# First loads of a two-block kernel in smaller pieces on two queues

## The chip, the cores and the metric

The kernel runs on one core of one Trainium2 chip. The metric is the device time of one execution in microseconds (us). A profiled execution gives a trace of every engine's instructions and of the DMA packets; its times count from the start of the span, the stretch from the first to the last instruction.

## The reference

The reference computes two transformer-like blocks on 256 tokens of width 1024, in float32, and a last norm. What matters here is the first work that the kernel does, the keys and values of the memory attention in the first block:

```
m = rms_norm(mem, mem_norm[l])                 # mem: 256 x 1024
mk, mv = jnp.split(m @ w_mem_kv[l], 2, axis=-1)
```

and what rms_norm is:

```
y = x32 * lax.rsqrt(jnp.mean(x32 * x32, axis=-1, keepdims=True) + EPS)
return (y * gain.astype(jnp.float32)).astype(x.dtype)
```

Everything after it (the recurrent, linear-attention and memory branches, both feed-forward parts, the second block) is untouched by the change.

## The kernel before

All activations lie with channels on the 128 partitions: mem is a tile memr of 128 x 8 x 256, channel tile k of 8 against 256 tokens. Weights lie in one packed array; the chunk memk0 is 8 channel tiles by 256 output columns, so 2048 numbers per partition, and memk1 and memk2 follow it.

Products are made three times over: every operand is split into a high part (rounded to the format that TensorE takes) and a low part (the rest). The helper split has ScalarE write the high part (line 156, or line 159 with a scale) and VectorE the low part (line 157 or 160). The helper mm3 issues high x high, high x low and low x high (lines 203 to 205). For mem the scale is the norm's gain, 8 columns named g_mem in the parameter tile par; the 1/rms of each token is worked out beside the products and multiplied in afterwards.

The opening goes as follows. A tile of ones is written; the first 16 columns of par (g_mem and g_mix) are loaded on ScalarE's queue; 13 products of ones by ones (line 258) run on TensorE before there is data. Then a loop over four quarters q loads on SP's queue two channel tiles of mem (mem_part, line 344) and the matching quarter of memk0 and of memk1 (512 columns each, line 363), splits each, and issues the 24 products of the quarter into two accumulators, fps[0] and fps[1]. Behind the loop come memk2 in quarters (line 191), the constants, the squares of mem (Ssq.add, lines 282 and 290), their fold (line 292), the column sums on TensorE (line 297), an inverse square root on VectorE (lines 306 to 321), and memk2's products. After that, weights are loaded in whole chunks (line 178), three raw buffers ahead.

The order written in the program is a priority. When the kernel is built, a planner puts each engine's instructions in an order by its own estimate of readiness, and so a square of mem can stand ahead of a weight's split that the program writes earlier. An engine keeps this order at run time, whatever is ready. In the trace the ninth load waits, at its issue, for the first one, that of the scales, to land.

Of the kernel before, what the change touches and what calls it, by code (L numbers as in the profile page):

```python
# [9 lines left out]
F32 = mybir.dt.float32  # L10
# [7 lines left out]
P = 128  # L18
D = 1024
S = 256  # L20
KT = D // P
# [25 lines left out]
NPAR = _o  # L47
# [18 lines left out]
WMAX = KT * 272  # L66
# [21 lines left out]
def wplan():  # L88
    plan = []
    for n in ("memk", "memv", "mq", "zrnn"):  # L90
        plan += [(f"{n}{j}", KT, 256) for j in range(3)]
    plan += [(f"qk{j}", KT, 256) for j in range(3)]
    plan += [("rga", 14, 128), ("rgx", 14, 128)]
    plan += [("v0", KT, 272), ("v1", KT, 256), ("v2", KT, 256)]
    plan += [(f"g{j}", KT, 256) for j in range(3)]
    for b in BR_ORDER:
        for j in range(4):
            plan += [(f"gate{b}_{j}", KT, 256), (f"br{b}_{j}", MT, 256)]
    plan += [(f"wout{j}", KT, 256) for j in range(4)]
    plan += ffn_plan("up", "dn", NF)  # L100
    plan += [(n, KT, IN2_WIDTH.get(n, 256)) for n in IN2_ORDER]
    plan += [(f"wo2_{j}", 2, 1024) for j in range(4)]
    plan += ffn_plan("gu", "dn2_", NF2)
    off = {}
    o = 0
    for n, a, b in plan:
        off[n] = (o, a, b)
        o += P * a * b
    return off, o


WOFF, WTOT = wplan()
# [3 lines left out]
def build(ctx: ExitStack, tc: tile.TileContext, ins: dict, out: bass.AP):  # L116
    nc = tc.nc
    act, dve, pool, pe = nc.scalar, nc.vector, nc.gpsimd, nc.tensor
    W = ins["w"]

    wrp = ctx.enter_context(tc.tile_pool(name="wrp", bufs=3))
    whp = ctx.enter_context(tc.tile_pool(name="whp", bufs=5))
    wlp = ctx.enter_context(tc.tile_pool(name="wlp", bufs=5))
    cp = ctx.enter_context(tc.tile_pool(name="cp", bufs=1))
# [8 lines left out]
    def uid(p):  # L133
        cnt[0] += 1
        return f"{p}_{cnt[0]}"

    def t2(shape=None, dt=F32):
        return tp.tile(shape or [P, 512], dt, tag="t2", name=uid("t2"))

    def slot(tag, shape, dt=F32):  # L140
        return sp.tile(shape, dt, tag=tag, name=uid(tag))

    def small(shape):
        n = uid("sm")
        return sm.tile(shape, F32, tag=n, name=n)

    def bank(shape=None):
        return psp.tile(shape or [P, 2, 256], F32, tag="ps", name=uid("ps"))
# [5 lines left out]
    def split(dst_h, dst_l, src, scale=None):  # L154
        if scale is None:
            act.activation(dst_h, src, AF.Copy)  # L156
            dve.tensor_tensor(dst_l, src, dst_h.bitcast(F32), op=ALU.subtract)  # L157
        else:
            act.activation(dst_h, src, AF.Identity, scale=scale)
            dve.scalar_tensor_tensor(dst_l, src, scale, dst_h.bitcast(F32),  # L160
                                     op0=ALU.mult, op1=ALU.subtract)
# [3 lines left out]
    raws = {}  # L165
# [36 lines left out]
    def mm3(o, lh, ll, rh, rl, start, stop, skip=False):  # L202
        pe.matmul(o, lh, rh, start=start, stop=False, skip_group_check=skip)  # L203
        pe.matmul(o, lh, rl, start=False, stop=False, skip_group_check=skip)  # L204
        pe.matmul(o, ll, rh, start=False, stop=stop, skip_group_check=skip)  # L205
# [43 lines left out]

    ones = cp.tile([P, P], F32, name="ones")  # L250
    dve.memset(ones, 1.0)
    par = cp.tile([P, NPAR], F32, name="par")
    nc.scalar.dma_start(par[:, :16], ins["par"][:, :16])
    warm = cp.tile([P, 1], F32, name="warm")
    act.activation(warm, ones[:, 0:1], AF.Identity)
    wps = aup.tile([P, P], F32, tag="aux", name="wps")
    for _ in range(13):
        pe.matmul(wps, ones, ones, start=True, stop=True)
    memr = slot("R1", [P, KT, S])
    xT = slot("R0", [P, KT, S])  # L260
    cst = cp.tile([P, NCST], F32, name="cst")

    def pv(name, i=0, n=1, rows=P):
        o, c = POFF[name]
        return par[:rows, o + i:o + i + n]

    def cv(name):
        o, c = COFF[name]
# [35 lines left out]
    def mean_eps(src, n, dst=None):  # L304
        v = dst if dst is not None else small(src.shape)
        dve.tensor_scalar(v, src, 1.0 / n, EPS, op0=ALU.mult, op1=ALU.add)
        return v

    def rsqrt(v):

        y = small(v.shape)
        h, t = (sm.tile(v.shape, F32, tag=f"rs{q}_{v.shape[-1]}", name=uid("rs")) for q in "ht")
        dve.tensor_scalar(y.bitcast(I32), v.bitcast(I32), -0.5, 1597463007.0, op0=ALU.mult, op1=ALU.add)
        dve.tensor_tensor(h, y, y, op=ALU.mult)
        dve.scalar_tensor_tensor(h, h, -0.5, v, op0=ALU.mult, op1=ALU.mult)
        dve.scalar_tensor_tensor(y, h, 1.5, y, op0=ALU.add, op1=ALU.mult)
        dve.tensor_tensor(h, y, y, op=ALU.mult)
        dve.tensor_tensor(h, h, v, op=ALU.mult)
        dve.tensor_scalar(t, h, 0.375, -1.25, op0=ALU.mult, op1=ALU.add)
        dve.tensor_tensor(t, t, h, op=ALU.mult)  # L320
        dve.scalar_tensor_tensor(y, t, 1.875, y, op0=ALU.add, op1=ALU.mult)
        return y
# [16 lines left out]
    mh = slot("H2", [P, KT, S], F32R)  # L339
    ml = slot("H3", [P, KT, S], F32R)  # L340
    m = (mh, ml)

    def mem_part(i):
        nc.sync.dma_start(memr[:, 2 * i:2 * i + 2, :], ins["memT"][:, 2 * i:2 * i + 2, :])
        for k in (2 * i, 2 * i + 1):
            split(mh[:, k, :], ml[:, k, :], memr[:, k, :], pv("g_mem", k))


    first = ("memk0", "memk1")
    fps = [bank(), bank()]  # L350
    fw = {}
    for q in range(4):
        mem_part(q)
        for n, name in enumerate(first):
            if q == 0:
                raws[name] = wrp.tile([P, WMAX], F32, tag="raw", name=uid("raw"))
            if q % 2 == 0:
                fw[n] = (whp.tile([P, WMAX // 2], F32R, tag="wh", name=uid("wh")),
                         wlp.tile([P, WMAX // 2], F32R, tag="wl", name=uid("wl")))
            o = WOFF[name][0]  # L360
            cr = slice(512 * q, 512 * q + 512)
            c = slice(512 * (q % 2), 512 * (q % 2) + 512)
            nc.sync.dma_start(raws[name][:, cr],
                              W[o:o + P * 2048].rearrange("(p n) -> p n", p=P)[:, cr])
            split(fw[n][0][:, c], fw[n][1][:, c], raws[name][:, cr])
            for k in range(2):
                for mo in range(2):
                    w0 = c.start + k * 256 + mo * P
                    kk = 2 * q + k
                    mm3(fps[n][:, mo, :], fw[n][0][:, w0:w0 + P], fw[n][1][:, w0:w0 + P],  # L370
                        mh[:, kk, :], ml[:, kk, :], kk == 0 and mo == 0, kk == KT - 1, skip=True)
    nxt[0] = 4
    c0, c1 = fps
# [8 lines left out]
    emit_half()  # L382
    for i in range(2):
        nc.sync.dma_start(xT[:, 4 * i:4 * i + 4, :], ins["xT"][:, 4 * i:4 * i + 4, :])
    nc.sync.dma_start(par[:, 16:], ins["par"][:, 16:])
    rm_tok = rsqrt(mean_eps(sm_.total(), D))
    xh = slot("H0", [P, KT, S], F32R)
    xl = slot("H1", [P, KT, S], F32R)
# [3 lines left out]
    def x_part(i):  # L392
        for k in (2 * i, 2 * i + 1):
            split(xh[:, k, :], xl[:, k, :], xT[:, k, :], pv("g_mix", k))
        sx.add(i, flat(xT[:, 2 * i:2 * i + 2, :]))
# [46 lines left out]


    lam = pv("rg_lam", 0, 6)
    c8 = small([P, 6])
    nc8 = small([P, 6])
# [156 lines left out]
    for j in range(3):  # L603
# [3 lines left out]
        for mi in range(2):  # L607
# [5 lines left out]
            while r < end:  # L613
                hd, p0 = divmod(r, DK)
                n = min(DK - p0, end - r)
# [190 lines left out]
    for bi, b in enumerate(BR_ORDER):  # L806
# [4 lines left out]
        for j in range(4):  # L811
# [4 lines left out]
            o = (outa, outb, outc)[b]  # L816
# [410 lines left out]
    for i, name in enumerate(IN2_ORDER):  # L1227
# [27 lines left out]
        elif i == 6:  # L1255
            for j in range(4):
                c = slice(2 * j, 2 * j + 2)
# [75 lines left out]
    for t in range(2):  # L1333
        ssq = small([P, 2])
        o = [t2(), t2()]
# [4 lines left out]
        v, r, q = small([P, 1]), small([P, 1]), small([P, 1])  # L1340
# [7 lines left out]
        rows = slice(t * P, (t + 1) * P)  # L1348
# [4 lines left out]
        else:  # L1353
            act.activation(o[0], o[0], AF.Copy, scale=r)
            nc.scalar.dma_start(out[rows, 0:512], o[0])
            for i in range(2):
                c = slice(256 * i, 256 * i + 256)
# [22 lines left out]
def pack(inp):  # L1380
    g = {k: np.asarray(v) for k, v in inp.items()}
# [75 lines left out]
    par = np.concatenate([pars[n] for n, _ in PAR_COLS], axis=1).astype(f32)  # L1457
# [12 lines left out]
    cst2 = np.concatenate([am, cntr.reshape(P, 512), pw], axis=1)  # L1470

    def tT(a):
        return np.ascontiguousarray(np.asarray(a, f32)[0].reshape(S, KT, P).transpose(2, 1, 0))

    return {
        "w": w, "par": np.ascontiguousarray(par), "cst": np.ascontiguousarray(cst),
        "cst2": np.ascontiguousarray(cst2), "xT": tT(g["x"]), "memT": tT(g["mem"]),
        "gdw": np.ascontiguousarray(g["gla_w_decay"]),
        "nf": np.ascontiguousarray(rep(g["norm_final_2"])),
    }  # L1480
# [14 lines left out]
```

## Time and profile before

| what | value |
|---|---|
| median of 3 runs | 797.26 us (796.67 to 797.52) |
| profiled execution | 797.59 us |
| its span | 795.8 us |
| TensorE busy in the span | 785.1 us |
| VectorE busy | 598.6 us |
| ScalarE busy | 481.8 us |

The profiled execution's own time is 1.8 us longer than its span; the rest is launch and end. TensorE is busy nearly all the time. In the rows below, PE is TensorE's matmul side, DVE is VectorE, ACT is ScalarE, SP is SyncE; a trailing q is an engine's sequencer or DMA queue. A tile's name is printed without its number: R is memr, H is mem's high or low part, raw a loaded weight, wh and wl its parts, ps an accumulator, t a temporary.

### The profile page before, as it was taken

What the parts mean: (1) busy time and instruction counts of PE and PEld (TensorE: products, weight loads), DVE (VectorE), ACT (ScalarE), POOL (GpSimd) and SP (SyncE); (2) the same over time, 40 slices, a digit from 0 to 9 for tenths busy, and PEclk for the clock granted to TensorE, in tenths of its full rate; (3) what the DMA queues carried; (4) which work ended last, traced back from release to release, by engine and by line L of the source; (5) the groups of instructions that cost most, each with busy time, mean ns of one, the idle gap of its engine ahead of it and who ended that gap; (6) DMA issues with size and microseconds to landing.
All of it is one profiled execution on the core that took longest, in us unless ns stands there. A gap on an engine that the chain in (4) does not pass through costs nothing.

```text
span 795.8 us, 15612 instructions
## 1 busy us (share of the span) xinstructions
PE 785.1 (99%) x6460; PEld 760.9 (96%) x6460; DVE 598.6 (75%) x980; ACT 481.8 (61%) x770; POOL 10.2 (1%) x23
## 2 busy tenths in 40 slices
PE   8999999999999999999999999999999999999996
PEld 8999989999889999999999999999899999999995
DVE  6988757965667777898778887899898756656663
ACT  6845679964345555666556565768976544444443
POOL 0000110000000000000000000000000000000000
PEclk9999999999999999999999999999999999999999
DMA  8864544364445665366555555263174544555521
GB/s 281 305 229 152 175 133 176 114 231 140 144 142 201 203 213 204 110 243 228 171 203 207 173 204 198 103 257 113 49 268 157 215 181 167 203 200 180 205 106 53
DMA packets 23526, 144.03 MB, mean 181 GB/s; under 512 B 2896, under 2 KB 3424, under 8 KB 8480
## 3 DMA queue, kind: packets, MB, share of 16 engines
q1 hardware_dynamic: 22464, 140.98, 49.9%
q0 software_dynamic: 704, 1.80, 0.6%
q8 instruction: 50, 0.82, 0.4%
q10 hardware_dynamic: 288, 0.27, 0.1%
q14 instruction: 20, 0.16, 0.1%
HBM read 141.20 MB, written 1.05 MB: 179 GB/s over the span
## 4 chain that ended last, share of the span: by engine, by line
PE 91%; DVE 4%; ACT 3%; issue 1%; DMA 1%; DVEq 0%; SPq 0%; ACTq 0%
PE ps L203 23%; PE ps L204 22%; PE ps L205 22%; PE aux L203 6%; PE aux L205 6%; PE aux L204 5%; DVE wl L157 2%; PE aux L521 1%; PE ps L220 1%; PE ps L227 1%; PE ps L218 1%; DMA raw<-w 1%; ACT wh L156 1%; PE aux L720 1%; ACT L1154 0%
## 5 line engine op out<-in xcount | busy, mean ns | idle before, releaser
L157 DVE TENSOR_TENSOR wl<-raw,wh 128x1024 fp32r<-128x1024 f32 (+4 forms) x276 | 322.1, 1172 | 119.5 <-ACT wh L156 117.7
L156 ACT ACTIVATE wh<-raw 128x1024 fp32r<-128x1024 f32 (+4 forms) x276 | 277.9, 1015 | 207.2 <-PE ps L204 159.6
L203 PE MATMUL ps<-H,wh 128*128 128x256 f32 x1320 | 368.2, 279 | 1.2 <-ACT wh L156 1.2
L205 PE MATMUL ps<-H,wl 128*128 128x256 f32 x1320 | 366.3, 278 | 0.2 <-DVE wl L157 0.2
L204 PE MATMUL ps<-H,wh 128*128 128x256 f32 x1320 | 366.3, 278 | 0.0
L203 PEld LDWEIGHTS ps<-H,wh 128*128 128x128 f32 x1320 | 248.0, 188 | 3.5 <-issue 1.8
L204 PEld LDWEIGHTS ps<-H,wh 128*128 128x128 f32 x1320 | 248.7, 188 | 0.3
L205 PEld LDWEIGHTS ps<-H,wl 128*128 128x128 f32 x1320 | 248.1, 188 | 0.4 <-DVE wl L157 0.4
L203 PE MATMUL ps<-wh,H 128*128 128x256 f32 (+2 forms) x192 | 54.6, 285 | 0.0
L204 PE MATMUL ps<-wl,H 128*128 128x256 f32 (+2 forms) x192 | 54.0, 281 | 0.3 <-DVE wl L157 0.3
L205 PE MATMUL ps<-wh,H 128*128 128x256 f32 (+2 forms) x192 | 54.1, 282 | 0.0
L205 PE MATMUL aux<-S,wl 128*128 128x256 f32 x192 | 53.1, 277 | 0.0
L204 PE MATMUL aux<-S,wh 128*128 128x256 f32 x192 | 53.1, 276 | 0.0
L203 PE MATMUL aux<-S,wh 128*128 128x256 f32 x192 | 53.1, 276 | 0.0
L156 ACT ACTIVATE S<-t 128x256 fp32r<-128x256 f32 x46 | 19.0, 415 | 50.3 <-DVE t L921 26.5
L543 DVE SCALAR_TENSOR_TENSOR t<-t,par,t 128x255 f32<-128x255 f32 (+1 forms) x96 | 40.1, 478 | 0.1
L204 PEld LDWEIGHTS ps<-wl,H 128*128 128x128 f32 x192 | 36.1, 188 | 0.5 <-DVE wl L157 0.5
L203 PEld LDWEIGHTS ps<-wh,H 128*128 128x128 f32 x192 | 36.1, 188 | 0.4 <-issue 0.4
L205 PEld LDWEIGHTS ps<-wh,H 128*128 128x128 f32 x192 | 36.1, 188 | 0.0
L205 PEld LDWEIGHTS aux<-S,wl 128*128 128x128 f32 x192 | 36.1, 188 | 0.0
L203 PEld LDWEIGHTS aux<-S,wh 128*128 128x128 f32 x192 | 36.1, 188 | 0.0
L204 PEld LDWEIGHTS aux<-S,wh 128*128 128x128 f32 x192 | 36.1, 188 | 0.0
(327 smaller groups left out, 1070.8 us busy)
## 6 DMA issues: line engine op xcount, KB each, us to landing
raw<-w SPq DMA_DIRECT2D x115, 1024.0 KB, 4.8
raw<-w SPq DMA_DIRECT2D x12, 768.0 KB, 4.3
raw<-w SPq DMA_DIRECT2D x12, 256.0 KB, 5.3
raw<-w SPq DMA_DIRECT2D x2, 896.0 KB, 4.5
raw<-w SPq DMA_DIRECT2D x1, 1088.0 KB, 6.2
raw<-w SPq DMA_DIRECT2D x1, 1048.0 KB, 4.8
R<-memT SPq DMA_DIRECT2D x4, 256.0 KB, 5.5
R<-xT SPq DMA_DIRECT2D x2, 512.0 KB, 8.8
```

The costliest lines, as they stand in the source:

```text
L156: act.activation(dst_h, src, AF.Copy)
L157: dve.tensor_tensor(dst_l, src, dst_h.bitcast(F32), op=ALU.subtract)
L203: pe.matmul(o, lh, rh, start=start, stop=False, skip_group_check=skip)
L204: pe.matmul(o, lh, rl, start=False, stop=False, skip_group_check=skip)
L205: pe.matmul(o, ll, rh, start=False, stop=stop, skip_group_check=skip)
L218: pe.matmul(ps[:, m, :], wh[:, k, c], x[0][:, kk, :], start=kk == 0 and m == 0, stop=False, skip_group_check=True)
L220: pe.matmul(ps[:, m, :], wl[:, k, c], x[0][:, kk, :], start=False, stop=False, skip_group_check=True)
L227: pe.matmul(ps[:, m, :], wh[:, k, m * P:(m + 1) * P], x[1][:, kk, :], start=False, stop=kk == nk - 1, skip_group_check=True)
L521: pe.matmul(ps[r0:r1, :], mv[:, mt, hd * DV + d0:hd * DV + d0 + r1 - r0], pts[hd][:, mt, :], start=mt == 0, stop=mt == 1, skip_group_check ...
L543: dve.scalar_tensor_tensor(dst[:, s:], src[:, :S - s], w(width - 1 - s), dst[:, s:], op0=ALU.mult, op1=ALU.add)
L720: pe.matmul(ps[:DK, i, :], kt[r, n // 2, hd * DK:(hd + 1) * DK], gv[r, n // 2, hd * DV:(hd + 1) * DV], start=True, stop=True)
```

## The change

The 16 scale columns are put in front of mem in device memory, so that each partition's row of memT is 16 scales and 2048 numbers of mem. The tile memr becomes the tail of a tile memall with 16 columns more; par loses its first 16 columns and its early load. The first quarter is loaded in smaller pieces and on two queues: on SP's queue the scales with channel tile 0 of mem (272 columns), then channel tile 1 (256), then memk1's first 512 columns; on ScalarE's queue memk0's first 512 columns in two pieces of 256. For q = 0 and memk0 the splits and the products go piece by piece: tile 0 of mem and columns 0 to 255 of memk0, six products, then tile 1 and columns 256 to 511, six products. The other quarters are loaded and split as before. The warm-up has 10 products in place of 13.

```diff
--- before.py
+++ after.py
@@ -249,20 +249,36 @@
 
     ones = cp.tile([P, P], F32, name="ones")
     dve.memset(ones, 1.0)
-    par = cp.tile([P, NPAR], F32, name="par")
-    nc.scalar.dma_start(par[:, :16], ins["par"][:, :16])
+    par = cp.tile([P, NPAR - 16], F32, name="par")
+
+    memall = slot("R1", [P, 16 + KT * S])
+    memr = memall[:, 16:].rearrange("p (k s) -> p k s", k=KT)
+    first = ("memk0", "memk1")
+    for n in first:
+        raws[n] = wrp.tile([P, WMAX], F32, tag="raw", name=uid("raw"))
+
+    def first_w(queue, name, c):
+        o = WOFF[name][0]
+        queue.dma_start(raws[name][:, c], W[o:o + P * 2048].rearrange("(p n) -> p n", p=P)[:, c])
+
+    nc.sync.dma_start(memall[:, :272], ins["memT"][:, :272])
+    for k in range(2):
+        first_w(nc.scalar, "memk0", slice(256 * k, 256 * k + 256))
+    nc.sync.dma_start(memr[:, 1, :], ins["memT"][:, 272:528])
+    first_w(nc.sync, "memk1", slice(0, 512))
     warm = cp.tile([P, 1], F32, name="warm")
     act.activation(warm, ones[:, 0:1], AF.Identity)
     wps = aup.tile([P, P], F32, tag="aux", name="wps")
-    for _ in range(13):
+    for _ in range(10):
         pe.matmul(wps, ones, ones, start=True, stop=True)
-    memr = slot("R1", [P, KT, S])
     xT = slot("R0", [P, KT, S])
     cst = cp.tile([P, NCST], F32, name="cst")
 
     def pv(name, i=0, n=1, rows=P):
         o, c = POFF[name]
-        return par[:rows, o + i:o + i + n]
+        if o < 16:
+            return memall[:rows, o + i:o + i + n]
+        return par[:rows, o - 16 + i:o - 16 + i + n]
 
     def cv(name):
         o, c = COFF[name]
@@ -340,33 +356,34 @@
     ml = slot("H3", [P, KT, S], F32R)
     m = (mh, ml)
 
-    def mem_part(i):
-        nc.sync.dma_start(memr[:, 2 * i:2 * i + 2, :], ins["memT"][:, 2 * i:2 * i + 2, :])
-        for k in (2 * i, 2 * i + 1):
-            split(mh[:, k, :], ml[:, k, :], memr[:, k, :], pv("g_mem", k))
-
-
-    first = ("memk0", "memk1")
+
+
     fps = [bank(), bank()]
     fw = {}
     for q in range(4):
-        mem_part(q)
+        ks = (2 * q, 2 * q + 1)
+        if q > 0:
+            nc.sync.dma_start(memr[:, ks[0]:ks[1] + 1, :],
+                              ins["memT"][:, 16 + 512 * q:16 + 512 * q + 512].rearrange("p (a b) -> p a b", a=2))
+            for k in ks:
+                split(mh[:, k, :], ml[:, k, :], memr[:, k, :], pv("g_mem", k))
         for n, name in enumerate(first):
-            if q == 0:
-                raws[name] = wrp.tile([P, WMAX], F32, tag="raw", name=uid("raw"))
             if q % 2 == 0:
                 fw[n] = (whp.tile([P, WMAX // 2], F32R, tag="wh", name=uid("wh")),
                          wlp.tile([P, WMAX // 2], F32R, tag="wl", name=uid("wl")))
-            o = WOFF[name][0]
-            cr = slice(512 * q, 512 * q + 512)
-            c = slice(512 * (q % 2), 512 * (q % 2) + 512)
-            nc.sync.dma_start(raws[name][:, cr],
-                              W[o:o + P * 2048].rearrange("(p n) -> p n", p=P)[:, cr])
-            split(fw[n][0][:, c], fw[n][1][:, c], raws[name][:, cr])
+            c0 = 512 * (q % 2)
+            if q > 0:
+                first_w(nc.sync, name, slice(512 * q, 512 * q + 512))
+            if q > 0 or n > 0:
+                split(fw[n][0][:, c0:c0 + 512], fw[n][1][:, c0:c0 + 512], raws[name][:, 512 * q:512 * q + 512])
             for k in range(2):
+                kk = 2 * q + k
+                if q == 0 and n == 0:
+                    c = slice(256 * k, 256 * k + 256)
+                    split(mh[:, kk, :], ml[:, kk, :], memr[:, kk, :], pv("g_mem", kk))
+                    split(fw[n][0][:, c], fw[n][1][:, c], raws[name][:, c])
                 for mo in range(2):
-                    w0 = c.start + k * 256 + mo * P
-                    kk = 2 * q + k
+                    w0 = c0 + k * 256 + mo * P
                     mm3(fps[n][:, mo, :], fw[n][0][:, w0:w0 + P], fw[n][1][:, w0:w0 + P],
                         mh[:, kk, :], ml[:, kk, :], kk == 0 and mo == 0, kk == KT - 1, skip=True)
     nxt[0] = 4
@@ -382,7 +399,7 @@
     emit_half()
     for i in range(2):
         nc.sync.dma_start(xT[:, 4 * i:4 * i + 4, :], ins["xT"][:, 4 * i:4 * i + 4, :])
-    nc.sync.dma_start(par[:, 16:], ins["par"][:, 16:])
+    nc.sync.dma_start(par, ins["par"][:, 16:])
     rm_tok = rsqrt(mean_eps(sm_.total(), D))
     xh = slot("H0", [P, KT, S], F32R)
     xl = slot("H1", [P, KT, S], F32R)
@@ -1474,7 +1491,7 @@
 
     return {
         "w": w, "par": np.ascontiguousarray(par), "cst": np.ascontiguousarray(cst),
-        "cst2": np.ascontiguousarray(cst2), "xT": tT(g["x"]), "memT": tT(g["mem"]),
+        "cst2": np.ascontiguousarray(cst2), "xT": tT(g["x"]), "memT": np.concatenate([par[:, :16], tT(g["mem"]).reshape(P, KT * S)], axis=1),
         "gdw": np.ascontiguousarray(g["gla_w_decay"]),
         "nf": np.ascontiguousarray(rep(g["norm_final_2"])),
     }
```

## Rows read from the trace of the kernel before

**Rows 1.** The page: its first line, and busy time by engine.

```profile
span 795.8 us, 15612 instructions
...
PE 785.1 (99%) x6460; PEld 760.9 (96%) x6460; DVE 598.6 (75%) x980; ACT 481.8 (61%) x770; POOL 10.2 (1%) x23
```

**Rows 2.** Waits of PE, whole span: us in total, times, longest.

```profile
PE aux L1086 <- ACT S L1154: 1.4, 1, 1.4
PE ps L203 <- ACT wh L156: 1.2, 1, 1.2
...
PE ps L204 <- DVE wl L157: 0.3, 1, 0.3
PE aux L297 <- DVE t L292: 0.2, 1, 0.2
```

**Rows 3.** Timeline of PE to 20 us: start, length, what, [idle before].

```profile
1.06 4.65 PE L258 MATMUL wps<-ones 128*128 128x128 f32 x26 [1.06 <-DVE ones L251]
...
4.32 1.39 PE L258 MATMUL wps<-ones 128*128 128x128 f32 x11
...
6.88 0.39 PE L203 MATMUL ps<-H,wh 128*128 128x256 f32 x1 [1.18 <-ACT wh L156]
...
7.61 0.39 PE L205 MATMUL ps<-H,wl 128*128 128x256 f32 x1 [0.22 <-DVE wl L157]
...
19.20 0.60 PE L297 MATMUL aux<-ones,t 128*128 128x1 f32 x4 [0.24 <-DVE t L292]
```

**Rows 4.** Timeline of DVE to 20 us.

```profile
5.81 0.88 DVE L160 SCALAR_TENSOR_TENSOR H<-R,par,H 128x256 fp32r<-128x256 f32 x2 [4.80 <-ACT H L159]
...
7.91 0.69 DVE L157 TENSOR_TENSOR wl<-raw,wh 128x512 fp32r<-128x512 f32 x1 [0.35 <-ACT wh L156]
...
18.72 0.42 DVE L292 TENSOR_TENSOR t<-t 128x256 f32<-128x256 f32 x1
```

**Rows 5.** The chain that ended last, 0 to 20 us: start, length, what.

```profile
1.17 5.01 DMA raw<-w
...
6.83 0.52 ACT t L282
```

**Rows 6.** DMA issues from 0.7 to 1.15 us: count, KB, us to landing.

```profile
R<-memT SPq DMA_DIRECT2D x1, 256.0 KB, 4.3
par<-par ACTq DMA_DIRECT2D x1, 8.0 KB, 4.5
```

**Rows 7.** DMA issues from 1.62 to 1.72 us.

```profile
raw<-w SPq DMA_DIRECT2D x1, 256.0 KB, 5.3
```

**Rows 8.** SP's queue to 12 us: an issue row of its timeline, one of its waits.

```profile
1.17 0.89 SPq L363 DMA_DIRECT2D raw<-w  x2
...
SPq L363 <- DMA par<-par: 1.0, 1, 1.0
```

**Rows 9.** DMA issues of the whole span: the output's smaller stores.

```profile
out_dram<-t SPq DMA_DIRECT2D x2, 128.0 KB, 2.1
```

**Rows 10.** Two stretches: busy us of PE, PEld, DVE, ACT, POOL, then clock, DMA share, GB/s.

```profile
2.00:4.50 2.50, 2.50 (x15) 2.50 (x14) 0.00 (x0) 0.67 (x2) 0.00 (x0) 1.00 0.81 162
...
6.00:14.00 8.00, 6.89 (x56) 6.69 (x57) 7.47 (x15) 7.97 (x18) 0.00 (x0) 1.00 1.05 389
```

**Rows 11.** DMA queues from 2.0 to 4.5 us: packets, MB, share of 16 engines.

```profile
q1 hardware_dynamic: 209, 0.39, 75.5%
q10 hardware_dynamic: 137, 0.01, 3.6%
```

**Rows 12.** Timeline of ACT to 9 us.

```profile
0.74 0.41 ACTq L253 DMA_DIRECT2D par<-par  x1
...
2.48 0.20 ACT L255 ACTIVATE warm<-ones 128x1 f32<-128x1 f32 x1
5.26 0.91 ACT L159 ACTIVATE H<-R,par 128x256 fp32r<-128x256 f32 x2 [2.59 <-DMA par<-par]
...
7.26 0.62 ACT L156 ACTIVATE wh<-raw 128x512 fp32r<-128x512 f32 x1
```

## Prediction

> **What bounds the kernel now.** I read three views in this order: the page's busy times, TensorE's waits, and the engines' order of work in the opening, with the chain that ended last.
>
> The page shows TensorE busy for 785.1 of the 795.8 us [rows 1]. At most 10.7 us is there to win, however the work is arranged. TensorE's waits say where some of it lies: 1.2 us before the first real product, 0.2 us at the column sums of line 297, and later 1.4 us at line 1086 and 0.3 us at line 204 [rows 2]. The change edits the opening alone, so I read the opening closely.
>
> TensorE starts on warm-up products at 1.06, runs out of them at 5.71, stands idle, and does the first real product at 6.88 [rows 3]. It waits once more, for the low half of the first weights, until 7.61 (line 205). From there it works without a gap up to the column sums at 19.20, which start 0.24 us after TensorE came free: they wait for VectorE's line 292, which ended at 18.72 + 0.42 = 19.14 [rows 3, 4].
>
> So two clocks run in the opening. TensorE's starts at 7.61, VectorE's at 7.91. The chain leads to the latter: memk0's first block, issued at 1.17, lands at 1.17 + 5.01 = 6.18; ScalarE splits it, then does a square of line 282 (0.52 us of the chain), then splits memk1's first block; VectorE makes that block's low half at 7.91 [rows 4, 5], and from there the chain stays on VectorE to line 292. VectorE's clock ends last. What the change is worth is therefore read at 19.20, where both clocks meet, and not at the first product. After it TensorE hardly waits, so what is gained or lost there should be carried to the end.
>
> **The change part by part.**
>
> *First pieces.* Now 256 KB of mem land 4.3 us after 0.74, at 5.04, and 8 KB of scales 4.5 us after 0.74, at 5.24 [rows 6]. memk1's block is the second of two issues that take 0.89 us from 1.17 on, so it is issued at about 1.62 and lands 5.3 us later, at 6.92 [rows 7, 8]. After, two transfers issued at the same time by SP and by ScalarE bring 128 runs of 1,088 bytes (scales and mem's first eighth, 139 KB) and 128 runs of 1,024 bytes (half of memk0's block, 131 KB): 270 KB in 256 runs, where now mem and the scales are 270 KB in 256 runs. Bytes and runs being the same, I take the same landing, 5.1. The bounds: not before 0.74 + 2.1 = 2.84, by the fastest transfer of such a size in this trace, an output of 128 KB [rows 9]; not after 6.18, when memk0 lands now.
>
> The Trainium skill bears on this in "DMA: Bandwidth & Descriptors", section "Issuing engines are not separate DMA queues": transfers from different issuers run on the same 16 DMA engines and interleave, and a second issuer saves only issuing time. The trace agrees that they share: the main queue moved 162 GB/s while the scales' queue had packets under way, and 389 later [rows 10, 11]. By the rule the four small pieces are one stream, memk0's half could land as late as the last of them, and the first product would gain nothing.
>
> *TensorE's start.* From 5.1 on: ScalarE's split of a mem eighth has a step of 0.45 (two in 0.91) [rows 12]. Its split of 256 weight columns I put at 0.36, an estimate a little over half of the 0.62 for 512. The first product comes at about 5.9. VectorE's mem split starts 0.55 after ScalarE's (5.81 against 5.26 [rows 4, 12]), its weight half follows, and the low weights are there at about 6.45. TensorE's clock then starts 1.1 to 1.2 us earlier than 7.61.
>
> *Warm-up.* The 13 products show as 26 records. The last 11 begin at 4.32 and take 1.39 us, a step of 0.11; the 15 before took 3.26 us, a step of 0.22 [rows 3]. These are TensorE's two levels, 2.4 and 1.2 GHz, read from the steps, since the granted clock reads 1.00 in both stretches [rows 10]. Ten products are 20 records: the last begins at 4.32 + 4 x 0.11 = 4.76 and ends at 5.04. That blocks no product at 5.9, and the idle stretch is 0.9 us, shorter than the 1.17 of now, after which products went on at the higher level. So I cost this edit at nothing. If the data landed at 2.84, the warm-up's end near 4.9 would be the floor of TensorE's start.
>
> *VectorE's start.* This decides. It needs memk1's first block, and ahead of the end of that block there are the same bytes as now (8 + 3 x 256 KB), so I take the same landing, 6.92. ScalarE then splits it in 0.62 and VectorE starts 0.03 after that, as now (7.26 + 0.62 + 0.03 = 7.91) [rows 4, 12]: 7.57 in place of 7.91, a gain of 0.34 us. Before, ScalarE has to do mem's second eighth and memk0's second half; 532 KB are ahead of these, where 520 KB had landed at 6.18, so they land at about 6.2, and 0.45 + 0.3 of splitting ends at about 6.95, just in time. The two instructions more (one weight split in two, on both engines) fall into time in which VectorE waits now. The condition is that the square of line 282 does not again stand ahead of memk1's split in ScalarE's order. With it, VectorE starts at 6.95 + 0.52 + 0.62 + 0.03 = 8.12, a loss of 0.2. I take the gain, as the program writes the split first; both ends stay in the range.
>
> *Queues.* One transfer fewer for the scales, two more for the halves. SP's fifth weight issue, the ninth load in all, waits 1.0 us for the scales' landing [rows 8]; after, mem's third quarter is in that place and waits for the first piece, 5.1 in place of 5.24. ScalarE issues two transfers of 0.41 us ahead of its table load, where it has one; its warm activation, now over at 2.68 [rows 12], ends at 3.1, long before data at 5.1. With data at 2.84 it would hold them by 0.3.
>
> *Sum.* The profiled execution took 797.59 us, 1.8 more than its span. Less 0.34 it is 797.25. The runs' median, 797.26, is 0.33 under the profiled execution, so the forecast for the median is 796.9.
>
> **Rivals.**
>
> 1. *The sums move.* The column sums come later in TensorE's order, or line 292 earlier in VectorE's, since the order is made anew at the build. Then TensorE's 1.1 and the 0.24 of waiting can come through: up to 1.3 us, 796.0. For it: products are ready earlier, VectorE's sums hardly. Against it: the program asks for the sums ahead of memk2's products.
>
> 2. *Early landing.* From 2.0 to 4.5 the DMA engines were 81% busy and moved 162 GB/s [rows 10]; in that stretch the scales' queue put 137 packets between 209 of the main queue [rows 11]. If those packets slow the main queue, the first blocks come sooner: the first piece at 2.84 at the earliest, the other 650 KB at 389 GB/s 1.7 us later, so memk1 between 4.5 and 6.92. At half way, 5.7, VectorE starts at 6.4: 1.5 us gained, 795.8. The skill's page named above, section "Specifications", speaks for it: runs under 512 bytes (the scales' are 64) cost a read-modify-write. No run here shows the opening without such runs. Against it: those packets are 8 KB in all, and a cold start could slow the same stretch without them.
>
> 3. *Small runs slow the opening; slower than now.* If in the cold stretch each packet counts alike, whatever its size (209 + 137 in 2.5 us, 138 per us [rows 11]), then 640 runs stand ahead of memk1's landing (four times 128 of about 1 KB, 128 of 2 KB), against 512 now. 128 more at 138 per us are 0.9 us: memk1 lands at 7.85, VectorE starts at 8.5, 0.6 later than now: 797.9. It decides once memk1 lands after 7.26, when ScalarE takes it now.
>
> 4. *No effect.* Interleaving holds memk0's half to 6.2, or the square keeps its place: 797.1 to 797.5.
>
> 5. *The clock.* If ten products don't bring the higher level, as much time at the lower one as now (3.26 us) would fall on real products: 1.6 us lost, 1.1 to 1.3 of it covered by TensorE's earlier start, 797.6.
>
> **How the numbers follow.** Forecast 0.42 (796.6 to 797.1 is its own range), rival 1 0.17, rival 2 0.13, rival 3 0.08, rival 4 0.15, rival 5 0.05. Leaving out the far half of rival 2, the whole of rival 3 and the tail of rival 1 joined with 2 gives 795.6 to 797.7. A measurement of this kernel tells about 0.2%, 1.6 us, from no change. Faster than 795.67 takes the far half of rival 2, or rivals 1 and 2 together: 0.11. Slower than 798.85 takes rivals 3 and 5 together, or an order later in the kernel that turns out badly: 0.04. Within: 0.85.
>
> **What the next profile would show.** The first real product near 5.9; VectorE's low half of memk1's first block near 7.6; line 292 ending near 18.8; a wait of about 1 us, not 0.24, at line 297. If that wait is gone it is rival 1; memk0's half in before 4.5 is rival 2; memk1's block after 7.3 is rival 3; products at a step of 0.22 is rival 5. What would make the forecast wrong above all is another order on TensorE around the sums.

## The result, and the profile after

The kernel with the change takes 804.25 us (median of 4 runs, 803.16 to 804.5), the kernel before 797.39 in the runs beside it: a ratio of 1.0085 (95% interval 1.0073 to 1.0096). It is slower, by 6.9 us. The forecast was 796.9 within 795.6 to 797.7, so it was wrong in sign and in size. The profiled execution of the change took 803.16 us, the lowest of the four.

The page of the changed kernel, against [rows 1]:

```profile
span 801.4 us, 15603 instructions
...
PE 791.3 (99%) x6454; PEld 767.3 (96%) x6454; DVE 600.1 (75%) x981; ACT 481.3 (60%) x771; POOL 10.2 (1%) x23
```

The span has grown by 5.6 us and TensorE's busy time by 6.2, with six matmul records fewer (the three warm-up products). So the loss is not waiting: the same products took longer. TensorE's waits after, against [rows 2], say the same: the 1.2 us before the first real product are gone, the sums' wait has grown from 0.2 to 0.8 us, and 0.2 us at line 343 (327 before) are new:

```profile
PE aux L1103 <- ACT S L1171: 1.4, 1, 1.4
PE wps L273 <- DVE ones L251: 1.1, 1, 1.1
PE aux L313 <- DVE t L308: 0.8, 1, 0.8
PE ps L204 <- DVE wl L157: 0.3, 1, 0.3
PE aux L343 <- DVE sm L337: 0.2, 1, 0.2
```

**The opening** came sooner than forecast. Timelines of TensorE, then of ScalarE and VectorE, in the changed kernel (line 313 was 297, 308 was 292, 273 was 258), against [rows 3, 4, 12]:

```profile
1.06 4.64 PE L273 MATMUL wps<-ones 128*128 128x128 f32 x20 [1.06 <-DVE ones L251]
5.34 0.56 PE L203 MATMUL ps<-H,wh 128*128 128x256 f32 x1
5.70 0.41 PE L204 MATMUL ps<-H,wh 128*128 128x256 f32 x1
...
19.02 0.61 PE L313 MATMUL aux<-ones,t 128*128 128x1 f32 x4 [0.75 <-DVE t L308]
```

```profile
3.49 0.51 ACT L159 ACTIVATE H<-R 128x256 fp32r<-128x256 f32 x1 [0.33 <-DMA R<-memT]
3.91 0.40 ACT L156 ACTIVATE wh<-raw 128x256 fp32r<-128x256 f32 x1
...
6.94 0.69 DVE L157 TENSOR_TENSOR wl<-raw,wh 128x512 fp32r<-128x512 f32 x1 [0.68 <-ACT wh L156]
...
18.55 0.42 DVE L308 TENSOR_TENSOR t<-t 128x256 f32<-128x256 f32 x1
```

The first piece is taken at 3.49 instead of 5.26, VectorE's low half of memk1's block comes at 6.94 instead of 7.91, and the column sums at 19.02 instead of 19.20. The sums alone would show a gain of 0.2 us. But in the changed kernel they also stand five products later in TensorE's order (101 real products ahead of them, 96 before), so TensorE has done more work by then. What it has gained is read at instructions that have the same work ahead of them. The rows below are the transposes at 25, 48 and 324 us and a product near 505 us, first of the kernel before, then the same four of the changed one (line 343 was 327):

```profile
25.20 0.38 PE L327 MATMUL aux<-cst,sm 128*128 128x128 f32 x2
48.48 0.38 PE L327 MATMUL aux<-cst,sm 128*128 128x128 f32 x2
324.96 0.38 PE L327 MATMUL aux<-cst,sm 128*128 128x128 f32 x2
504.95 0.28 PE L203 MATMUL ps<-wh,H 128*128 128x262 f32 x1
```

```profile
24.46 0.38 PE L343 MATMUL aux<-cst,sm 128*128 128x128 f32 x2
48.10 0.43 PE L343 MATMUL aux<-cst,sm 128*128 128x128 f32 x2 [0.20 <-DVE sm L337]
323.57 0.38 PE L343 MATMUL aux<-cst,sm 128*128 128x128 f32 x2
510.37 0.29 PE L203 MATMUL ps<-wh,H 128*128 128x262 f32 x1
```

So the opening gained 0.7 us; at 48 us, where TensorE now waits for VectorE, 0.4 of it is left. At 324 us the changed kernel is 1.4 us ahead, and at the last row 5.4 us behind.

**Where the time went.** TensorE alone in four stretches, first of the kernel before, then of the changed one (busy us, records, granted clock, DMA share, GB/s):

```profile
130.00:335.00 205.00, 205.00 (x1732) 1.00 0.49 172
335.00:505.00 170.00, 170.00 (x1502) 1.00 0.55 193
505.00:560.00 55.00, 54.95 (x473) 1.00 0.50 183
560.00:760.00 200.00, 198.37 (x1542) 1.00 0.50 181
```

```profile
130.00:335.00 205.00, 205.00 (x1740) 1.00 0.50 172
335.00:505.00 170.00, 170.00 (x1446) 1.00 0.54 193
505.00:560.00 55.00, 55.00 (x472) 1.00 0.46 164
560.00:760.00 200.00, 198.28 (x1558) 1.00 0.51 181
```

From 335 to 505 us TensorE is busy without a gap in both and the granted clock reads 1.00 in both, yet one issues 1,502 products and the other 1,446: one every 113.2 ns against one every 117.6. The 56 products missing are worth 6.3 to 6.6 us, which is the loss, less small gains elsewhere (8 products more from 130 to 335 us are 0.9). The DMA engines are no busier. How the step changes can be watched. TensorE's timeline before, around 331 us, and of the changed kernel at the same time:

```profile
330.62 0.28 PE L204 MATMUL ps<-H,wh 128*128 128x256 f32 x1
...
331.10 0.28 PE L205 MATMUL ps<-H,wl 128*128 128x256 f32 x1
331.21 0.28 PE L203 MATMUL ps<-H,wh 128*128 128x256 f32 x1
331.32 0.28 PE L204 MATMUL ps<-H,wh 128*128 128x256 f32 x1
331.44 0.28 PE L205 MATMUL ps<-H,wl 128*128 128x256 f32 x1
331.55 0.28 PE L203 MATMUL ps<-H,wh 128*128 128x256 f32 x1
```

```profile
330.88 0.28 PE L203 MATMUL ps<-H,wh 128*128 128x256 f32 x1
...
331.58 0.28 PE L203 MATMUL ps<-H,wh 128*128 128x256 f32 x1
```

Read the starts, not the lengths. Before, five steps from 330.62 to 331.21 are 0.59 us, three from 331.21 to 331.55 are 0.34: the step falls from 118 to 113 ns between two products of the same lines, and stays there for some 1,530 products, up to 504.95 us. In the changed kernel it goes on at 117 to 118 (six steps, 0.70 us), up to 510.37 us.

**What in the diff can reach 331 us?** No work, only places. The order of TensorE's products, which the prediction named as the chief danger, is the same in both traces but for the sums and one pair at 545 us. The tile par is 64 bytes per partition narrower. In the compiled program the constants tile cst, whose first 128 columns are the identity used in the transposes of line 327, and mem's slot R1 behind it start 64 bytes lower; R1 is 64 bytes longer, so every tile behind it keeps its place. And the kernel has a table that the text has not spoken of so far:

```python
for _n in ("up3", "xbc3", "gu6"):
    PLACE[_n, 0] = 28
    PLACE[_n, 1] = 30
```

It shifts the parts of three weight chunks inside their buffers by 28 and 30 numbers. The step of before falls right behind the 48 products of up3.

### The profile page after: what moved, and what is told of

Read it like the earlier page. It is cut to its first block, busy times and chain, and to the rows that moved or that the text cites. A ratio compares the mean times of both kernels' runs of the same rounds, so it can differ in the third digit from the quotient of the medians.

```text
span 801.4 us, 15603 instructions
## 1 busy us (share of the span) xinstructions
PE 791.3 (99%) x6454; PEld 767.3 (96%) x6454; DVE 600.1 (75%) x981; ACT 481.3 (60%) x771; POOL 10.2 (1%) x23
## 4 chain that ended last, share of the span: by engine, by line
PE 89%; DVE 4%; ACT 2%; issue 2%; DMA 1%; SPq 0%; DVEq 0%; ACTq 0%
PE ps L203 22%; PE ps L204 22%; PE ps L205 22%; PE aux L203 6%; PE aux L204 6%; PE aux L205 6%; DVE wl L157 1%; DMA raw<-w 1%; PE aux L538 1%; PE ps L220 1%; PE ps L218 1%; PE ps L227 1%; ACT wh L156 1%; PE aux L737 1%; ACT L1171 0%
## 5 line engine op out<-in xcount | busy, mean ns | idle before, releaser
L203 PE MATMUL aux<-S,wh 128*128 128x256 f32 x192 | 54.0, 281 | 0.0
L204 PE MATMUL aux<-S,wh 128*128 128x256 f32 x192 | 54.0, 281 | 0.0
```

## The experiments

Two theories stood against each other first. *Warm-up and opening* (theories N and T below): fewer warm-up products, or other timing of the first 20 us, leave TensorE in another condition. *Places* (theory A): the narrower tile moves the constants. Each run below is compared with runs of the kernel before on the same chip, and its ratio to them stands with a 95% interval. The four-digit number is the count of products from 335 to 505 us.

**The warm-up count** (the changed kernel with 13, the kernel before with 10).

```diff
-    for _ in range(10):
+    for _ in range(13):
```

> The changed kernel with 13 warm-up products again. Theory N (the count of TensorE's instructions ahead of the work sets the step of its products later): the step between 335 and 505 us goes back to 113 ns (about 1,500 products in that stretch) and the time to 796 or 797 us. Theories A (addresses moved by 64 bytes) and T (the pieces' arrival and the order in the opening): no change, 1,446 products and 803 to 804.5 us.

> The kernel before with 10 warm-up products and nothing else changed. Theory N: the slow step of 117.6 ns appears between 335 and 505 us, 1,446 products there, 802 to 804 us. Theories A and T: no change, 1,502 products and 796.7 to 797.7 us; TensorE starts its first real product at 6.9 as before.

With 13 the changed kernel takes 804.5 us, ratio 1.0092 (1.0077 to 1.0107), 1,446 products: nothing is undone. With 10 the kernel before takes 797.95 (796.3 to 799.11, 10 runs), 1.0009 (1.0000 to 1.0019), and keeps its 1,502. The warm-up count isn't the cause of the loss.

**The places, forward and back.** First the change with par as wide as before, which puts the constants back, but moves all slots behind R1 up by 64 bytes; then the kernel before without the shifts of PLACE.

```diff
-    par = cp.tile([P, NPAR - 16], F32, name="par")
+    par = cp.tile([P, NPAR], F32, name="par")[:, :NPAR - 16]
```

> The changed kernel, but the parameter tile keeps the 16 unused columns, so that the constants lie where they lay before; the tiles behind mem's slot lie 64 bytes higher. Theory A for the constants (ident, read by the transposes): the step goes back to 113 ns between 335 and 505 us, 796 to 797 us. Theories N and T: 117.6 ns, 803 to 804.5 us.

```diff
-for _n in ("up3", "xbc3", "gu6"):
+for _n in ():
```

> The kernel before without the shifts of 28 and 30 numbers that three weight chunks (up3, xbc3, gu6) have within their buffers; same arithmetic. If those shifts are what brings TensorE from the step of 117.6 to that of 113 ns at about 331 us, the slow step stays from 320 to 505 us: 1,446 products there and 803 us or more. If the step has nothing to do with them: 1,502 products and 797 us.

The one took 825.84 us, 1.0361 (1.0346 to 1.0377), the other 804.02 (2 runs), 1.0087 (1.0067 to 1.0108). The stretch from 335 to 505 us in both:

```profile
335.00:505.00 170.00, 170.00 (x1419) 1.00 0.53 182
```

```profile
335.00:505.00 170.00, 170.00 (x1446) 1.00 0.55 193
```

The undoing made it worse: with the activation tiles 64 bytes up, a step of 119.8 ns (170 us over 1,419). And the kernel before without its shifts is just as slow as the changed one, with the same count. So the change looks as if it switched off what PLACE brings. Next, the kernel before with nothing changed but places:

```diff
-    par = cp.tile([P, NPAR], F32, name="par")
-    nc.scalar.dma_start(par[:, :16], ins["par"][:, :16])
+    par = cp.tile([P, NPAR - 16], F32, name="par")
...
     cst = cp.tile([P, NCST], F32, name="cst")
+    head = cp.tile([P, 16], F32, name="head")
+    nc.scalar.dma_start(head, ins["par"][:, :16])
```

> The kernel before, but the first 16 parameter columns have a small tile of their own behind the constants, so that the constants (and the one-column warm tile) lie 64 bytes lower, as in the changed kernel, and every other tile lies where it lay. The loads, their order and the 13 warm-up products are those of before. Theory A (the place of the constants, which the transposes read ahead of the feed-forward products): about 1,446 products in TensorE between 335 and 505 us, 803 to 804.5 us. Theory T (the new loads and their order in the opening): 1,502 products there and 796.7 to 797.7 us. A third theory, that mem's slot 64 bytes lower is the cause, also gives 797.

This took 804.38 us, 1.0092 (1.0079 to 1.0105):

```profile
335.00:505.00 170.00, 170.00 (x1445) 1.00 0.55 193
```

That is the whole loss, with the old loads, the old pieces and 13 warm-up products. The other way round, the change with every tile where it was before (the scales again loaded apart; pieces, two queues and 10 warm-up products kept):

```diff
-    par = cp.tile([P, NPAR - 16], F32, name="par")
+    par = cp.tile([P, NPAR], F32, name="par")
+    nc.scalar.dma_start(par[:, :16], ins["par"][:, :16])
...
-    memall = slot("R1", [P, 16 + KT * S])
-    memr = memall[:, 16:].rearrange("p (k s) -> p k s", k=KT)
+    memr = slot("R1", [P, KT * S]).rearrange("p (k s) -> p k s", k=KT)
```

> The changed kernel with the scales loaded apart as before, first on ScalarE's queue, and mem without them, so that every tile lies at the address of before. Pieces, two queues, order and 10 warm-up products are those of the change. Theory A: 1,502 products between 335 and 505 us and a time of 796.5 to 797.3, which shows what the opening is worth; with 64-byte runs at its head memk0's first half lands later than the 3.9 us of the changed kernel, by up to 1 us. Theory T: 1,446 products there and 803 to 804.5 us.

It took 797.54 us (796.43 to 800.26, 12 runs), 1.0011 (1.0001 to 1.0021):

```profile
335.00:505.00 170.00, 170.00 (x1502) 1.00 0.55 193
```

So places take the time and places give it back. This run also tests rival 2, since the scales' 64-byte runs are back at the head of ScalarE's queue. Its ScalarE, against 3.49 and 3.91 in the changed kernel:

```profile
3.65 0.51 ACT L159 ACTIVATE H<-R,par 128x256 fp32r<-128x256 f32 x1
5.76 0.42 ACT L156 ACTIVATE wh<-raw 128x256 fp32r<-128x256 f32 x1 [1.60 <-DMA raw<-w]
```

From 2.0 to 4.5 us all queues together moved 239 GB/s in the changed kernel, then 150 in this one:

```profile
2.00:4.50 2.50, 2.50 (x14) 2.50 (x13) 0.47 (x2) 1.96 (x4) 0.00 (x0) 1.00 0.91 239
2.00:4.50 2.50, 2.50 (x14) 2.50 (x13) 0.31 (x1) 1.99 (x3) 0.00 (x0) 1.00 0.76 150
```

With the 64-byte runs back, mem's first piece still comes early (3.65), so it doesn't need their absence; memk0's half, behind the scales on ScalarE's queue, comes late.

**Which tile.** The identity alone 64 bytes lower, its masks in place (the scales fill the gap); then the whole constants tile 32 bytes lower.

```diff
-CST_COLS = [("ident", 128), ("tri", 128), ("gmask", 128)]
+CST_COLS = [("ident", 128), ("scales", 16), ("tri", 128), ("gmask", 128)]
```

> The kernel before with the identity matrix alone 64 bytes lower (and the one-column warm tile); the two masks of the constants lie where they lay, the gap between holds the scales, and the constants are loaded in two transfers. If the transposes' reading of the identity sets the step (theory A, the narrow form): about 1,446 products between 335 and 505 us, 803 to 804.5 us. If it is the masks: 1,502 and 797.

```diff
     nc.scalar.dma_start(par[:, :16], ins["par"][:, :16])
+    cst = cp.tile([P, NCST], F32, name="cst")
     warm = cp.tile([P, 1], F32, name="warm")
```

> The kernel before with the constants 32 bytes lower and nothing else moved but the one-column warm tile. It tells how fine the dependence on the constants' place is: 797 us and 1,502 products between 335 and 505 us if 32 bytes are the same as none; 803 to 804.5 and 1,446 if any move undoes the setting that the shifts of up3 had been chosen for.

The first took 805.14 us, 1.0099 (1.0085 to 1.0113), with 1,446 products: it is the identity that counts. (The parameter columns behind the scales move by 64 bytes with it, but so they do in the mended change below, which has 1,502.) The second took 797.62, 1.0001 (0.9991 to 1.0011), with 1,502: 32 bytes don't matter.

**The activation tiles.** Unused bytes behind the constants move all activation tiles up: 64, 32, and 128 in the changed kernel. Two small tiles of the last norm are merged to make room for 64 and 128.

```diff
     cst = cp.tile([P, NCST], F32, name="cst")
+    gap = cp.tile([P, 16], F32, name="gap")
+    dve.memset(gap, 0.0)
```

> The kernel before with 64 unused bytes between the constants and mem's slot, so that all activation tiles lie 64 bytes higher and the weights and constants where they lay (two small tiles of the last norm share one to make room). If addresses alone gave the 825.8 us of the changed kernel with the wide parameter tile: 820 us or more, a step of 120 ns (about 1,417 products between 335 and 505 us). If that took the new loads as well: 797 to 798 us.

> The kernel before with all activation tiles 32 bytes higher, weights and constants in place. Against the 826 us at 64 bytes higher: 810 to 815 us if the step grows with the distance, 797 if only a move of 64 bytes or more counts, 826 if half a line is as bad as a line.

> The changed kernel with its own loads, padded so that the constants and mem's slot lie where they lay before and all tiles behind that slot 128 bytes higher, not 64 (two small tiles of the last norm share one to make room). Theory A with a period of 128 bytes or less: 1,502 products between 335 and 505 us, 796.5 to 797.3 us. Theory A with a period of 256 bytes: another level, 800 us or more. Theory T: 803 to 804.5 us.

By 64 bytes: 826.45 us (2 runs), 1.0371 (1.0353 to 1.0389). By 32: 818.62 (2 runs), 1.0269 (1.0250 to 1.0288). By 128, constants and R1 where they were before: 811.79, 1.0189 (1.0176 to 1.0203). The three stretches, in that order:

```profile
335.00:505.00 170.00, 170.00 (x1420) 1.00 0.52 181
```

```profile
335.00:505.00 170.00, 170.00 (x1439) 1.00 0.53 185
```

```profile
335.00:505.00 170.00, 170.00 (x1445) 1.00 0.55 191
```

So the activation tiles' place accounts for the 825.84 of the wide par, and no period of 128 bytes brings the short step back.

**The change without its loss.** A cut of par in two puts the constants 256 bytes lower than before and every activation slot in its old place; mem's slot still starts 64 bytes lower.

```diff
-    par = cp.tile([P, NPAR - 16], F32, name="par")
+    PSP = POFF["cb2"][0]
+    par = cp.tile([P, PSP - 16], F32, name="par")
+    cst = cp.tile([P, NCST], F32, name="cst")
+    par2 = cp.tile([P, NPAR - PSP], F32, name="par2")
...
-    nc.sync.dma_start(par, ins["par"][:, 16:])
+    nc.sync.dma_start(par, ins["par"][:, 16:PSP])
+    nc.sync.dma_start(par2, ins["par"][:, PSP:])
```

> The changed kernel with its own loads and 10 warm-up products; the parameters are cut into two tiles so that the constants lie 256 bytes lower than before (192 lower than in the change) and every activation tile behind mem's slot where it lay before. Theory A with a period of 256 bytes: 1,502 products between 335 and 505 us, and the time shows what the change's opening is worth: by the profile of the changed kernel, where the sums at the end of the opening came about 0.2 us sooner, 796.5 to 797.2. Theory A without a period (each address its own): any level, 800 us or more if slow. If mem's slot, still 64 bytes lower, mattered: 803.

797.42 us (795.86 to 798.57, 11 runs), 0.9998 (0.9989 to 1.0007), 1,502 products; the first real product at 5.34 as in the change. The loss is gone, mem's slot plays no part, and of the opening's gain nothing can be measured. Its profile shows where the gain went. TensorE comes to the transposes of 25.20 at 24.59, 0.6 us ahead, and then waits 0.40 us for VectorE at those of 48.48; and from 50 to 70 us it issues 172 products against 179 in the kernel before. The kernel before with 10 warm-up products, where no tile has moved, has 172 there as well, so this is not a matter of places alone.

**Against each other or each by itself?** The constants 128 and 192 bytes lower by the same kind of cut (at dtb and at cb2) in the kernel before; 64 unused bytes ahead of every tile; and the mended change with the activation tiles 32 bytes lower.

```diff
+    gp = ctx.enter_context(tc.tile_pool(name="gp", bufs=1))
     wrp = ctx.enter_context(tc.tile_pool(name="wrp", bufs=3))
...
+    gap = gp.tile([P, 16], F32, name="gap")
+    dve.memset(gap, 0.0)
```

> The kernel before with 64 unused bytes ahead of every tile, so that weights, identity and activation tiles all lie 64 bytes higher and none has moved against another; two small tiles of the last norm are merged to make room. If the step of the products is set by the tiles' places against each other, nothing changes: 797.5 us, 1,502 products from 335 to 505 us. If it is set by each place by itself (within 256 bytes, say), the activation tiles' move of 64 bytes should cost what it cost alone, 820 to 827 us.

> The kernel before, with the last 31 columns of the parameters in a tile of their own behind the constants, so that the constants alone lie 128 bytes lower; loads, pieces, warm-up products and every other place as before. If the identity's place counts by 256 bytes and only its own old place brings the short step behind up3, this is as slow as the shift by 64 bytes: 804 us, some 1,446 products from 335 to 505 us. If what counts is whether the shift is an odd or an even number of 64-byte lines, it stays at 797.5 us with 1,502 products.

> As the kernel with the constants 128 bytes lower, but 192 bytes lower (64 bytes higher within 256). If only the old place within 256 bytes brings the short step: 804 us and some 1,446 products from 335 to 505 us. If an odd number of 64-byte lines is what loses it: 804 us too; if 64 bytes lower is the one bad place: 797.5 us and 1,502 products.

```diff
-    par2 = cp.tile([P, NPAR - PSP], F32, name="par2")
+    par2 = cp.tile([P, NPAR - PSP + 1], F32, name="par2")
...
-    warm = cp.tile([P, 1], F32, name="warm")
+    warm = par2[:, NPAR - PSP:]
```

> The change with the constants 256 bytes lower and, besides, the activation tiles behind them 32 bytes lower than in the kernel before. Moving them up by 32 and by 64 bytes raised the step nearly everywhere (818.6 and 826.5 us). If the step grows with the distance in one direction, moving them down shortens it: below 795 us, with a step under 113 ns somewhere. If the old place is the best of its neighbours, it comes out slower: 800 to 819 us.

Everything up by 64: 797.5 us, 1.0003 (0.9994 to 1.0012), 1,502 products. The activation tiles' same move alone had cost 29 us. So places count against each other, and a move of 64 bytes that weights, identity and activations share costs nothing.

Constants 192 bytes lower: 797.46, 1.0001 (0.9992 to 1.0011), 1,502 products; both forecasts of a loss fell. Constants 128 lower: 799.95 with a spread of 796.36 to 800.36 over 10 runs, 1.0019 (1.0004 to 1.0035). The ten fall in two groups, four of 796.4 to 796.6 and six of 799.9 to 800.4. In the profile, of one of the six, the short step holds behind up3 (1,503), but an earlier stretch has fewer products; of the kernel before, then of this one:

```profile
270.00:318.00 48.00, 48.00 (x426) 1.00 0.59 208
```

```profile
270.00:318.00 48.00, 48.00 (x410) 1.00 0.57 197
```

Of the five shifts, then, 32, 192 and 256 bytes cost nothing that can be measured, 64 costs the stretch behind up3, and 128 costs some executions another stretch; I find no simple period in that. The activation tiles 32 bytes lower: 816.85, 1.0248 (1.0233 to 1.0264), 1,451 products. Both neighbours of the old place are worse, and the version that was to beat both kernels is no such version.

## Why the prediction was wrong

**The step that failed** is the last sentence of the first part: "After it TensorE hardly waits, so what is gained or lost there should be carried to the end." TensorE hardly waits, that is right, and 0.7 us were gained; but being carried to the end takes products that follow each other as fast as before, and the some 1,530 behind up3 came 4.4 ns later each. The part-by-part working has a price for every load, split and product that the diff touches, and none for the tile par, whose width is the first line of the diff. It was costed at nothing without a sentence, and the 64 bytes by which it moves the identity were worth 6.9 us. A loss clear of noise was given 0.04, for other reasons. The same step failed in a smaller way too: a TensorE that is ahead meets waits that the kernel before didn't have, and one for VectorE, at 48 us, left only 0.4 of the 0.7 us.

*Rival 5* was the near one, since it has slower products in it, but it puts them on the warm-up. Thirteen warm-up products changed nothing (1,446 both times), and where the products are slow the granted clock reads 1.00. *Rival 1* came in part: the sums stand five products later, which is 0.6 us of TensorE's work at 0.118 each.

*First pieces*: forecast to land at 5.1, taken at 3.49 and 3.91. "Bytes and runs being the same, I take the same landing" is the term that was mis-sized. Rival 2, the early landing, happened, but the cause named there explains only half of it. The smaller piece of mem comes early with or without the scales' 64-byte runs (3.65 and 3.49). memk0's half does not: with those runs at the head of ScalarE's queue it was taken at 5.76 instead of 3.91, of which 0.44 us is its later issue. The Trainium skill, "DMA: Bandwidth & Descriptors", section "Specifications", says that runs under 512 bytes pay a read-modify-write; this run agrees that such runs cost (150 GB/s against 239), though it cannot show by what. The same page of the Trainium skill, section "Issuing engines are not separate DMA queues", says that transfers of different issuers interleave on the same 16 DMA engines. What the prediction worked out from that for rival 4, memk0's half as late as the last piece, did not come (3.91, where 6.2 was feared). The 532 KB and the 520 KB of the working are the same bytes in two units (520 times 1,024), so the 6.2 doesn't change; and the 162 GB/s given there to the main queue are those of all queues (the main queue's own 0.39 MB in 2.5 us are 156).

*TensorE's start*: forecast 5.9, came at 5.34, and not on data, which was ready before 4.9: the warm-up products ended there. The forecast had the last five at a step of 0.11 us; the ten took 4.28 us in 20 records, 0.21 each to the end, and the first real products have the long step too (from 5.70 by 0.21).

*VectorE's start*: forecast 7.57, came at 6.94. Of this gain of 0.97 us on 7.91 only 0.17 is left at the fold (18.55 against 18.72), as VectorE then waited 0.35 and 0.18 us for ScalarE's splits and ran the same 21 instructions less closely packed. The sums waited 0.75 us; "about 1" was said.

*Sum*: the opening gave 0.7 us, 0.2 by VectorE's fold and the rest by the sums' later place, where 0.34 was forecast by the fold alone. So the forecast's own mechanism gave half of its size, and the opening was the wrong place to look for what decides.

**What stays open**: how places set the step inside TensorE. Shown is that they do, that the identity and the activation tiles count, and that they count against each other. From 335 to 505 us every profile agrees with that. With weights and activation tiles unmoved against each other, the five kernels with the constants 64 bytes lower or without PLACE have 1,445 or 1,446 products there, and the eight others have 1,502 or 1,503. Elsewhere places alone don't settle it: the kernel before without PLACE has every tile where it was, yet from 200 to 270 us, ahead of up3, it issues 586 products against 580 (587 in the changed kernel), and the ten executions with the constants 128 bytes lower fall in two groups 3.5 us apart. That the transposes, which read the identity, switch the step from one to the other is an inference from the tile that matters; the switch seen above at 331.2 lies some 50 products behind the two transposes at 324.96, not at them.

## What to carry to other kernels

A diff that changes the width of a tile changes the places of all that is allocated behind it, and that is an edit with a price of its own: list the tiles that move and hold them in place (a tile as wide as before, a pad, a tile cut in two) before the edit's own worth is measured. When busy time grows and waits don't, count the products per stretch at the same granted clock; a longer step at an unchanged order is not a matter of the schedule, and here it was the operands' places. Read a gain at an instruction that has the same work ahead of it in both kernels, not at one that the new order has moved. And a kernel with hand-set shifts of buffers, like PLACE here, is tuned to one set of places: each change of the layout needs the setting tried again.

## What the runs showed of the hardware

- Products of 256 columns ran, at a granted clock of 1.00, at steps of 113.2, 117.6 and 119.8 ns (170 us over 1,502, 1,446 and 1,419 products), held for hundreds of products on end. With the same products the kernel took from 797 to 826 us by where its tiles lay.
- A move of the constants, or of the identity in them alone, by 64 bytes cost 7 us (804.38 and 805.14). A move of the constants by 32, 192 or 256 bytes cost nothing that can be measured, and by 128 it cost some executions 3.5 us. A move of all tiles together by 64 bytes cost nothing, of the activation tiles alone 29 us.
- With 8 KB in 64-byte runs at the head of ScalarE's queue the DMA engines moved 150 GB/s from 2.0 to 4.5 us, and 239 where those bytes came in the 1,088-byte runs of mem's first piece.
- With ten warm-up products and the old, later loads the clock fell once products were under way. Stretches of that profile (the kernel before with 10):

```profile
7.00:9.00 2.00, 1.77 (x13) 0.92 1.06 383
9.00:11.00 2.00, 2.00 (x11) 0.50 1.04 389
```

From 9 to 11 us the granted clock is 0.50, the lower of the two levels (1.2 GHz), after TensorE had stood idle from 5.55 to 6.84. That is near to what rival 5 feared, but with the old loads; in the changed kernel TensorE did not stand idle there, and the granted clock reads 1.00.
